# Two heads of a chunk in one step: the score and value products of three attentions in a two-block transformer kernel

## The chip, the cores and the metric

The kernel runs on one core of one Trainium2 chip. The metric is device microseconds of one execution of the whole program, as the median of three runs. A core has engines that run side by side, each with its own queue: TensorE (PE in the profile; its weight loads are PEld), VectorE (DVE), ScalarE (ACT), GpSimd (POOL) and SyncE (SP), whose queue mostly issues transfers. Products are written to PSUM, which has banks of 128 partitions x 512 float32; the kernel uses eight of them, two under each of the names `mm`, `s`, `t` and `o`.

## The reference, cut to what matters

Two transformer blocks on one sequence of T = 512 tokens of width 1024, all in float32. The change touches three attentions, all with heads of 64. Block 1 has a neighbourhood attention (8 heads on an 8 x 64 grid of tokens) and a dilated one (4 heads for each of 3 groups, whose results are mixed by their log-sum). Each of the two layers of block 2 has a sliding-window attention with sinks (8 query heads, 2 key heads), between two other attentions. For the sliding window:

```python
s = einsum('bnqgrd,bnkgd->bngrqk', qb, kb) * dh ** -0.5        # scores, 128 queries x 256 keys
s = where(mask, s, NEG_INF)
p = softmax(concatenate([s, sink], -1), -1)[..., :-1]
o = einsum('bngrqk,bnkgd->bnqgrd', p, vb)                      # values
```

The other two have the same form with other masks, and with a bias added to the scores. Everything else (projections, gates, feed-forward parts, two more attentions in each layer) consists of dense products and is not changed.

## The kernel before, in words

Tensors stand with features on partitions. A "chunk" is 128 features, hence two heads of 64: head 0 on partitions 0 to 63, head 1 on partitions 64 to 127. Dense products (`gemm`, L143 to L145; `vals`, L535 to L537) split each float32 operand in two float32r parts and add three products of 128 x 128 weights with up to 512 columns. Their weights arrive by transfers in SP's queue and are split by ACT (L88) and DVE (L89).

An attention step for 128 queries of one head goes: score product into a bank `s`; maximum (DVE, with the bias added), exponential and row sum (ACT); the reciprocal; `halves` (L98 ACT, L99 DVE), which scales the probabilities and writes them as two float16 parts; `turn` (L105), which transposes each 128 x 128 block by a product with the identity into a bank `t`; `copy` (L820 on ACT and L822 on DVE, in turn) to a tile `pts`; and the value product into a bank `o`. Score and value operands of the two attentions of block 1, and the value operands of the sliding window, are plain float32: the trace shows two PE instructions for each such product. The score products of block 1 contract over the 64 partitions of one head (`hs`), so they use 64 rows of the array. The value products write the 64 partitions of one head in `po`, so they use 64 of its columns. The sliding window's score products contract over 128 partitions (two parts of a key stacked) and use the whole array.

- Neighbourhood (`mix1`, loop over `c` in 4 chunks, `hp` in 2 heads, `cb` in 4 blocks of queries): one score product (L593) of 256 columns into its own bank, then softmax, two blocks turned, a 256-column copy, two value products (L609). The bias comes by one transfer for each head (L587) into a tile `bias` of which there are two. `vb` has six tiles, which hold the dilated attention's bias (L619) and values (L627 to L635).
- Dilated, `dil_scores(jp)` for two chunks: for each group `g` the heads one after the other; group 0 has 256 keys for each block of queries (L694, L698, L699; two blocks fill a bank), groups 1 and 2 have 128 (L692, four blocks to a bank). `dil_values(jp)`: head by head, 512 columns of turned blocks to a bank, one copy, four value products (L764).
- Sliding window (`swa`, called in both layers): head by head; scores of four blocks of queries (L1314 to L1319), softmax, then two banks of turned blocks (three and four blocks), two copies, and the value products (L1353). After each head a generator step lets one chunk of a dense product (`gates`) in.

The program is written as a sequence. A scheduler orders each engine's instructions ahead of time by a simulated timeline: those earlier in the program first, and later ones where an earlier one has to wait for its data or for a free tile. So dense products that come later in the text fill PE between the steps of an attention. On the chip the order of each engine is fixed. The change and the prediction speak of L593, L609, L692 to L699, L764, L1353, L98, L99, L105, L587, L619 and L635.

Of the kernel before, what the change touches and what calls it, by code (L numbers as in the profile page):

```python
# [17 lines left out]
T = 512  # L18
# [3 lines left out]
UP = 2.0 ** 15  # probabilities go through the turn times UP, values are divided by it  # L22
# [4 lines left out]
class Core:  # L27
# [13 lines left out]
    @contextmanager  # L41
    def phase(self, name, **tags):
        """a pool within the pools that are open: tag -> (bufs, floats to a partition)"""
        outer = self.tags
        with self.tc.tile_pool(name=name, bufs=1) as p:
            self.tags = {**outer, **{k: (p, *v) for k, v in tags.items()}}
            yield
        self.tags = outer

    def t(self, tag, dt=F32, n=None):  # L50
        """a tile of an open phase"""
        p, bufs, size = self.tags[tag]
        x = p.tile([128, size], dt, name=tag, tag=tag, bufs=bufs)
        return x if n is None else x[:, :n]
# [29 lines left out]
    # ---- exact split of float32 into two float32r parts  # L84
# [9 lines left out]
    def halves(self, P, scale, w=T):  # L94
        """P * scale as a sum of two float16 tiles"""
# [6 lines left out]
    def turn(self, out, hl, cols):  # L102
        """out = (h + l)[:, cols] transposed"""
# [3 lines left out]
    # ---- weights: DRAM -> SBUF -> (hi, lo)  # L107
# [4 lines left out]
    def pieces(self, raw, kc, n, where=None):  # L112
        """([hi], [lo]) of each row block; `where`: pairs of tags instead of the usual tiles"""
# [13 lines left out]
    def wcols(self, w, c0, n, k0=0, kc=8, where=None):  # L127
        """columns [c0, c0+n) of w rows [k0*128, (k0+kc)*128): list of pieces, 128 columns each"""
# [8 lines left out]
    def gemm(self, ps, w, xh, xl, cols=ALL):  # L137
        """ps[m, t] = sum_k w[k, m] x[k, t] for the tokens of cols; w = pieces, xh, xl lists of [128, T]"""
# [8 lines left out]
    # ---- rms statistics of feature-major chunks  # L147
# [26 lines left out]
        # first guess by halving the exponent, then Newton's steps  # L174
# [92 lines left out]
# ---------------------------------------------------------------- shape-only constants  # L267
# [50 lines left out]
class Block1(Core):  # L318
# [14 lines left out]
    def load_gains(self, a, names, eng):  # L333
        """one row per 128 features, turned to columns"""
# [23 lines left out]
    def load_x(self, x, gname):  # L358
        """chunks of x, features on partitions, and the norm that follows"""
# [101 lines left out]
    def gates(self, w, uh, ul, R, n, name):  # L461
        """tanh(gate / 2) of n feature chunks, to DRAM; sigmoid(z) = (1 + tanh(z / 2)) / 2; yields after each chunk"""
# [12 lines left out]
    def branch(self, gd, w, O, hl, merged, mtag="x"):  # L475
        """merged += (1 + tanh(gate / 2)) * (o @ w); yields after each chunk"""
# [30 lines left out]
    def mix1(self, X, U, a):  # L507
# [9 lines left out]
        def vals_w(c0, where=(None, None)):  # L517
            """weights of the values of 256 columns"""
# [5 lines left out]
        def vals(sets, dst, ms=range(4), held=None):  # L524
            """tokens on partitions, to dst [512, 256 a set] in DRAM"""
# [22 lines left out]
        # ---- A: neighbourhood  # L548
# [31 lines left out]
        self.narrow()  # L580
        for c in range(4):
            po = self.bank("o")
            for hp in range(2):
                h = 2 * c + hp
                hs = slice(hp * 64, hp * 64 + 64)
                bias = self.t("bias")
                nc.sync.dma_start(bias, self.na_bias.rearrange("r c h v k -> (r c) h (v k)")[:, h])  # L587
                bias = bias.rearrange("p (v k) -> p v k", v=3)
                k3 = K[c][hs].rearrange("p (r c) -> p r c", c=64)
                for cb in range(4):  # L590
                    st = self.small(tag="sa")
# [3 lines left out]
                    s = self.t("p")  # L595
                    nc.vector.tensor_tensor_reduce(s[:, 0:256], ps[:, 0:256], bias[:, BVAR[cb]], 1.0, -3e38,
                                                   OP.add, OP.max, st[:, 0:1])
                    p = self.expo(s[:, 256:512], s[:, 0:256], st)
                    nc.vector.reciprocal(st[:, 3:4], st[:, 2:3])
                    nc.vector.tensor_scalar(st[:, 3:4], st[:, 3:4], UP, None, op0=OP.mult)  # L600
                    hl = self.halves(p, st[:, 3:4], 256)
                    pt = self.bank("t")
                    for i in range(2):
                        blk = slice(i * 128, i * 128 + 128)
                        self.turn(pt[:, blk], hl, blk)
                    pts = self.t("pts")
                    self.copy(pts[:, 0:256], pt[:, 0:256])
                    for i in range(2):
                        nc.tensor.matmul(po[hs, cb * 128:(cb + 1) * 128], V[cb][:, i, h * 64:(h + 1) * 64],  # L609
                                         pts[:, i * 128:(i + 1) * 128], start=i == 0, stop=i == 1)  # L610
# [4 lines left out]
        # ---- B: dilated mixture  # L615
# [22 lines left out]
        def perm(ap, g):  # L638
            """natural token order seen in the order of group g"""
# [9 lines left out]
        def lviews(L, g, x):  # L649
            """[(partitions, DRAM view [p, 4, x])] of the token axis of L in the order of group g"""  # L650
# [7 lines left out]
        def dil_scores(jp):  # L658
# [14 lines left out]
            for g in range(3):  # L673
                both = None
                for hp in range(2):
                    hs = slice(hp * 64, hp * 64 + 64)
                    j = 2 * jp + hp
                    q, k = QB[g][hs], KB[g][hs]
                    kw = 256 if g == 0 else 128
                    if g == 0:  # L680
                        pt = self.t("vw")
                    else:
                        both = self.t("vw") if hp == 0 else both
                        pt = both[:, hp * 512:hp * 512 + 512]
                    P[g, hp] = pt = pt.rearrange("p (t k) -> p t k", t=4)
                    for t0 in range(0, 4, 512 // kw):
                        ps = self.bank("s").rearrange("p (t k) -> p t k", k=kw)
                        for ti in range(512 // kw):
                            t = t0 + ti
                            qt = q[:, t * 128:(t + 1) * 128]  # L690
                            if g:
                                nc.tensor.matmul(ps[:, ti], qt, k[:, t * 128:(t + 1) * 128], start=True, stop=True)  # L692
                            elif t in (1, 2):
                                nc.tensor.matmul(ps[:, ti], qt, k[:, 128 * t - 64:128 * t + 192], start=True, stop=True)  # L694
                            else:
                                e = k.rearrange("p (b t) -> p b t", t=64)[:, 0:8:7, :]
                                m = k[:, 64:192] if t == 0 else k[:, 320:448]
                                nc.tensor.matmul(ps[:, ti, 0:128], qt, e if t == 0 else m, start=True, stop=True)  # L698
                                nc.tensor.matmul(ps[:, ti, 128:256], qt, m if t == 0 else e, start=True, stop=True)  # L699
                        for ti in range(512 // kw):  # L700
# [5 lines left out]
                            else:  # L706
# [3 lines left out]
                                                           mx[:, g, t, hp:hp + 1])  # L710
                    nc.vector.tensor_scalar(neg[:, g, :, hp], mx[:, g, :, hp], -1.0, None, op0=OP.mult)
# [32 lines left out]
        def dil_values(jp, P, coef):  # L744
            for g in range(3):
                po = self.bank("o")
                nk = 2 if g == 0 else 1
                for hp in range(2):
                    hs = slice(hp * 64, hp * 64 + 64)
                    j = 2 * jp + hp  # L750
# [830 lines left out]
```

## Time and profile before

| | us |
|---|---|
| median of three runs (lowest, highest) | 3314.46 (3313.63, 3319.1) |
| span of the profiled execution | 3312.9 |
| PE busy in it | 3235.0 (98%) |
| DVE busy | 1913.5 (58%) |
| ACT busy | 1479.6 (45%) |
| mean granted clock of TensorE | 0.988 |
| neighbourhood attention | about 470 to 572 |
| dilated attention | about 588 to 746 |
| sliding windows of the two layers | about 1568 to 1656 and 2586 to 2676 |

The profile is of one execution. Its page gives each engine's busy time. The view by stretch gives the same for parts of the span, the view by line groups instructions of one line and shape, the view of waits tells which instruction of an engine waited for which other one, and the chain of waits follows the end of the program back in time. Along PE the chain gives one piece for each run of instructions of one line: when the piece began and how long it lasted until the next piece. A matmul's end in the trace is modelled, so a busy PE is not yet a PE at its peak, and the length of a chain piece says more than a matmul's own duration.

### The profile page before, as it was taken

The numbers are of one execution on the slowest core, as the hardware profiler recorded it, in microseconds if no ns is written. First come the engines' busy times: TensorE is split into PE (matmuls) and PEld (weight loads), VectorE is DVE, ScalarE is ACT, GpSimd is POOL, SyncE is SP. The second block draws the span as 40 slices with busy tenths as digits, with TensorE's granted clock in tenths as the row PEclk, the third lists the DMA queues.
The fourth block names the chain that finished last, engine by engine and source line by source line (L and its number), as shares of the span: only waits on it lengthen the run. The fifth ranks groups of instructions, "written<-read, shape, count | busy, mean of one in ns | idle before, by whom it ended". The sixth has DMA issues, their size and how long they took to land.

```text
span 3312.9 us, 45062 instructions
## 1 busy us (share of the span) xinstructions
PE 3235.0 (98%) x16815; PEld 2654.6 (80%) x16815; DVE 1913.5 (58%) x3749; ACT 1479.6 (45%) x2933; POOL 356.8 (11%) x562
## 2 busy tenths in 40 slices
PE   8999999999899998999999999999999999999998
PEld 7888887778888887788777888888778778788887
DVE  5344655545644457777676544356677667544355
ACT  4322344543432334677665422234577667322233
POOL 3100321101570011000003000000000002100001
PEclk9999999999999998999999999999899999999999
DMA  4432253235233324332355332324433345423222
GB/s 136 138 98 92 86 177 98 83 101 188 83 106 98 99 81 139 83 115 94 106 168 189 108 101 90 102 86 135 110 90 107 105 142 185 144 94 97 95 90 70
DMA packets 373930, 373.41 MB, mean 113 GB/s; under 512 B 48640, under 2 KB 326016, under 8 KB 373712
## 3 DMA queue, kind: packets, MB, share of 16 engines
q1 hardware_dynamic: 366864, 358.48, 35.1%
q0 software_dynamic: 6640, 12.01, 1.3%
q8 instruction: 132, 2.16, 0.3%
q14 instruction: 86, 0.70, 0.1%
q10 hardware_dynamic: 208, 0.05, 0.0%
HBM read 320.16 MB, written 44.91 MB: 110 GB/s over the span
## 4 chain that ended last, share of the span: by engine, by line
PE 90%; DVE 4%; DMA 3%; ACT 1%; issue 1%; SPq 0%; POOL 0%; DVEq 0%; ACTq 0%; POOLq 0%
PE ps_mm L143 13%; PE ps_mm L144 13%; PE ps_mm L145 13%; PE ps_t L143 6%; PE ps_t L145 6%; PE ps_t L144 6%; PE ps_s L145 6%; PE ps_s L143 6%; PE ps_s L144 6%; PE ps_s L956 2%; PE ps_t L982 2%; PE ps_t L105 1%; PE ps_o L989 1%; PE ps_o L990 1%; PE ps_o L1353 1%
## 5 line engine op out<-in xcount | busy, mean ns | idle before, releaser
L88 ACT ACTIVATE whi<-wraw 128x1024 fp32r<-128x1024 f32 (+3 forms) x518 | 503.8, 977 | 1157.1 <-PE ps_mm L144 352.1
L89 DVE TENSOR_TENSOR wlo<-wraw,whi 128x1024 fp32r<-128x1024 f32 (+3 forms) x518 | 595.6, 1152 | 173.7 <-ACT whi L88 168.2
L143 PE MATMUL ps_mm<-uh,whi 128*128 128x512 f32 (+1 forms) x1616 | 636.7, 394 | 3.6 <-DVE ft L1028 1.9
L145 PE MATMUL ps_mm<-uh,wlo 128*128 128x512 f32 (+1 forms) x1616 | 631.5, 391 | 0.0
L144 PE MATMUL ps_mm<-ul,whi 128*128 128x512 f32 (+1 forms) x1488 | 582.6, 392 | 3.1 <-DVE ul L92 3.1
L143 PEld LDWEIGHTS ps_mm<-uh,whi 128*128 128x128 f32 x1616 | 305.3, 189 | 61.3 <-DVE ft L1028 2.8
L145 PEld LDWEIGHTS ps_mm<-uh,wlo 128*128 128x128 f32 x1616 | 304.6, 189 | 56.3 <-issue 0.2
L144 PEld LDWEIGHTS ps_mm<-ul,whi 128*128 128x128 f32 x1488 | 281.1, 189 | 55.2 <-DVE ul L92 3.8
L143 PE MATMUL ps_t<-uh,whi 128*128 128x512 f32 (+1 forms) x632 | 243.7, 386 | 0.0
L145 PE MATMUL ps_t<-uh,wlo 128*128 128x512 f32 (+1 forms) x632 | 242.8, 384 | 0.0
L144 PE MATMUL ps_t<-ul,whi 128*128 128x512 f32 (+1 forms) x632 | 242.7, 384 | 0.0
L144 PE MATMUL ps_s<-ul,whi 128*128 128x512 f32 (+1 forms) x544 | 208.7, 384 | 0.0
L145 PE MATMUL ps_s<-uh,wlo 128*128 128x512 f32 (+1 forms) x544 | 208.6, 383 | 0.0
L143 PE MATMUL ps_s<-uh,whi 128*128 128x512 f32 (+1 forms) x544 | 208.4, 383 | 0.0
L99 DVE SCALAR_TENSOR_TENSOR ph<-p,sa,ph 128x128 f16<-128x128 f32 (+2 forms) x224 | 124.4, 561 | 28.9 <-ACT ph L98 26.6
L143 PEld LDWEIGHTS ps_t<-uh,whi 128*128 128x128 f32 x632 | 120.5, 191 | 22.7 <-DVE ul L92 0.2
L145 PEld LDWEIGHTS ps_t<-uh,wlo 128*128 128x128 f32 x632 | 120.4, 190 | 22.6
L144 PEld LDWEIGHTS ps_t<-ul,whi 128*128 128x128 f32 x632 | 120.4, 191 | 22.5
L98 ACT ACTIVATE ph<-p,sa 128x128 f16<-128x128 f32 (+2 forms) x224 | 121.9, 555 | 27.5 <-DVE sa L977 15.7
L956 PE MATMUL ps_s<-k,q 128*128 128x256 f32 (+1 forms) x448 | 131.0, 377 | 2.1 <-ACT p L961 1.7
L961 ACT ACTIVATE p<-ps_s,sa 128x128 f32<-128x128 f32 (+1 forms) x192 | 100.9, 529 | 50.0 <-DVE sa L960 34.8
L143 PEld LDWEIGHTS ps_s<-uh,whi 128*128 128x128 f32 x544 | 103.1, 190 | 19.5
(666 smaller groups left out, 6365.2 us busy)
## 6 DMA issues: line engine op xcount, KB each, us to landing
wraw<-w_in_in SPq DMA_DIRECT2D x28, 1024.0 KB, 5.4
wraw<-w_branch_gate_in SPq DMA_DIRECT2D x24, 1024.0 KB, 6.1
wraw<-ffn_w_gate_in SPq DMA_DIRECT2D x22, 1024.0 KB, 5.3
wraw<-ffn_w_up_in SPq DMA_DIRECT2D x22, 1024.0 KB, 5.3
wraw<-w_ffn_gate_in SPq DMA_DIRECT2D x22, 1024.0 KB, 6.1
wraw<-w_ffn_up_in SPq DMA_DIRECT2D x22, 1024.0 KB, 5.3
wraw<-ffn_w_down_in SPq DMA_DIRECT2D x24, 768.0 KB, 4.6
gates<-gt SPq DMA_DIRECT2D x64, 256.0 KB, 2.1
```

The source lines that it names most:

```text
L88: nc.scalar.activation(hi, src, AF.Copy)
L89: nc.vector.tensor_tensor(lo, src, hi.bitcast(F32), op=OP.subtract)
L98: self.nc.scalar.activation(h, P, AF.Copy, scale=scale)
L99: self.nc.vector.scalar_tensor_tensor(l, P, scale, h, op0=OP.mult, op1=OP.subtract)
L105: self.nc.tensor.matmul(out, hl[e][:, cols], self.ident16, start=e == 0, stop=e == 1)
L143: nc.tensor.matmul(o, w[0][k], xh[k][:, cols], start=k == 0, stop=False)
L144: nc.tensor.matmul(o, w[0][k], xl[k][:, cols], start=False, stop=False)
L145: nc.tensor.matmul(o, w[1][k], xh[k][:, cols], start=False, stop=k == kc - 1)
L956: nc.tensor.matmul(ps[:, 0:n], l, r, start=i == 0, stop=i == len(mms) - 1)
L961: nc.scalar.activation(P[:, 0:w], ps[:, 0:w], AF.Exp, bias=st[:, 0:1], accum_out=st[:, 1:2])
L982: nc.tensor.transpose(pt[:, e, k], hl[e][:, k * 128:k * 128 + 128], self.ident16)
L989: nc.tensor.matmul(o, v, PH[:, k], start=first and k == 0, stop=False)
```

## The change

Both heads of a chunk go through one step. In the neighbourhood attention a step takes two blocks of queries and both heads: two banks `s`, one for each head, four score products that alternate between the heads; then for each block of queries the softmax of both heads, four turned blocks in one full bank `t`, one copy of 512 columns, and four value products that alternate between the heads. `dil_scores` fills two banks `s` for the two heads of a group with alternating products, and then works through their softmax; `dil_values` turns the blocks of both heads into one bank and alternates their value products. `swa` takes the heads in pairs: scores and softmax of one, a generator step, scores and softmax of the other, then for each of the four blocks of queries the turns of both heads in one bank, one copy and the alternating value products.

Tiles: the neighbourhood's bias goes to `vb` and the tag `bias` is gone; `p` has four tiles instead of two, `ph` four instead of three; the norm at the end of `mix1` takes its two scratch tiles from `p`. The rest of the diff removes docstrings and comments.

```diff
 # mix1, neighbourhood
+        pair = tuple(slice(64 * e, 64 * e + 64) for e in range(2))
         for c in range(4):
             po = self.bank("o")
-            for hp in range(2):
-                bias = self.t("bias")
...
-                for cb in range(4):
-                    ps = self.bank("s")
-                    nc.tensor.matmul(ps[:, 0:256], Q[c][hs, cb * 128:(cb + 1) * 128],
-                                     k3[:, :, WSTART[cb]:WSTART[cb] + 32], start=True, stop=True)
...
+                b = self.t("vb", n=768)
...
+            for cb0 in range(0, 4, 2):
+                ps = [self.bank("s") for _ in pair]
+                for cb in (cb0, cb0 + 1):
+                    for hp, hs in enumerate(pair):
+                        nc.tensor.matmul(ps[hp][:, cb % 2 * 256:cb % 2 * 256 + 256], Q[c][hs, cb * 128:(cb + 1) * 128],
+                                         k3[hp][:, :, WSTART[cb]:WSTART[cb] + 32], start=True, stop=True)
+                for cb in (cb0, cb0 + 1):
                     pt = self.bank("t")
+                    for hp in range(2):
...
+                        hl = self.halves(p, st[:, 3:4], 256)
+                        for i in range(2):
+                            self.turn(pt[:, hp * 256 + i * 128:hp * 256 + i * 128 + 128], hl, slice(i * 128, i * 128 + 128))
+                    pts = self.t("pts")
+                    self.copy(pts, pt)
                     for i in range(2):
+                        for hp, hs in enumerate(pair):
+                            nc.tensor.matmul(po[hs, cb * 128:(cb + 1) * 128], V[cb][:, i, h * 64:(h + 1) * 64],
+                                             pts[:, hp * 256 + i * 128:hp * 256 + i * 128 + 128], start=i == 0, stop=i == 1)
 # dil_scores
+                for t0 in range(0, 4, 512 // kw):
+                    banks = [self.bank("s").rearrange("p (t k) -> p t k", k=kw) for _ in pair]
+                    def heads(ti, lo, w, t, keys):
+                        for ps, hs in zip(banks, pair):
+                            nc.tensor.matmul(ps[:, ti, lo:lo + w], QB[g][hs, t * 128:(t + 1) * 128], keys(KB[g][hs]),
+                                             start=True, stop=True)
...
 # dil_values
+                nt = 2 // nk
+                for t0 in range(0, 4, nt):
+                    pt = self.bank("t").rearrange("p (t h n q) -> p t h n q", t=nt, h=2, q=128)
...
+                    for ti in range(nt):
+                        for i in range(nk):
+                            for hp, hs in enumerate(pair):
                                 nc.tensor.matmul(po[hs, t * 128:(t + 1) * 128], VB[g][:, m, j * 64:(j + 1) * 64],
+                                                 pts[:, ti, hp, i], start=i == 0, stop=i == nk - 1)
 # swa
+        for h0 in range(0, 8, 2):
+            for h in (h0, h0 + 1):
...
+                kept.append((P, st))
+                if h == h0:
+                    yield
+            po = self.bank("o")
+            for j in range(4):
+                nk = 2 if j else 1
+                pt = self.bank("t")[:, 0:256 * nk].rearrange("p (h n q) -> p h n q", h=2, q=128)
+                for e, (P, st) in enumerate(kept):
+                    hl = self.halves(P[:, j, 0:128 * nk], st[:, 4, j:j + 1], 128 * nk)
+                    for n in range(nk):
+                        self.turn(pt[:, e, n], hl, slice(n * 128, n * 128 + 128))
...
+                for n in range(nk):
+                    for e, r in enumerate(rows):
+                        nc.tensor.matmul(po[r, j * 128:(j + 1) * 128], v, pts[:, e, n], start=n == 0, stop=n == nk - 1)
 # tiles of mix1
-            with k.phase("mix1", q=(10, 512), vb=(6, 1024), bias=(2, 768), p=(2, 512), pts=(2, 512), gt=(2, 512),
-                         ob=(2, 512), r8=(1, 512), sc=(6, 32), stats=(2, 72), ph=(3, 512)):
+            with k.phase("mix1", q=(10, 512), vb=(6, 1024), p=(4, 512), pts=(2, 512), gt=(2, 512),
+                         ob=(2, 512), r8=(1, 512), sc=(6, 32), stats=(2, 72), ph=(4, 512)):
```

## Rows read from the trace of the kernel before

**Rows 1.** The page: busy time of each engine, share, instructions.

```profile
PE 3235.0 (98%) x16815; PEld 2654.6 (80%) x16815; DVE 1913.5 (58%) x3749; ACT 1479.6 (45%) x2933; POOL 356.8 (11%) x562
```

**Rows 2.** By stretch: length, busy PE, PEld, DVE, ACT, POOL, clock, DMA share, GB/s.

```profile
470.00:572.00 102.00, 102.00 (x681) 79.23 (x680) 58.19 (x222) 53.55 (x136) 11.17 (x20) 1.00 0.33 98
588.00:746.00 158.00, 156.96 (x858) 121.60 (x857) 82.88 (x259) 78.02 (x201) 14.40 (x24) 1.00 0.30 91
1568.00:1656.00 88.00, 86.75 (x566) 67.22 (x563) 56.08 (x134) 57.67 (x150) 0.95 (x5) 1.00 0.33 99
2586.00:2676.00 90.00, 88.99 (x577) 68.88 (x577) 60.26 (x142) 59.22 (x156) 1.16 (x6) 1.00 0.32 100
```

**Rows 3.** PE by line and shape, block 1's attentions: count, busy us, mean ns.

```profile
L593 PE MATMUL ps_s<-q 64*128 64x256 f32 x64 | 20.2, 416 | 0.0
L609 PE MATMUL ps_o<-pts,vw 128*64 128x128 f32 x128 | 18.7, 281 | 0.0
L764 PE MATMUL ps_o<-pts,vb 128*64 128x128 f32 x128 | 17.4, 279 | 0.0
```

**Rows 4.** By stretch, PE alone, writing the banks `s`: the dilated scores.

```profile
588.00:652.00 64.00, 16.62 (x112) 1.00 0.27 80
```

**Rows 5.** PE by line and shape, both layers: the sliding windows' value products.

```profile
L1353 PE MATMUL ps_o<-p,v 128*64 128x128 f32 x224 | 30.1, 280 | 0.7 <-ACT p L820 0.7
```

**Rows 6.** The chain, pieces by start, length, what: neighbourhood scores, dense beside them.

```profile
474.39 0.12 PE ps_mm L535
474.50 0.63 PE ps_s L593 x2
475.13 0.31 PE ps_mm L536
...
485.15 1.06 PE ps_s L593 x4
```

**Rows 7.** The chain: neighbourhood values of one head, and the dense product behind.

```profile
519.99 0.58 PE ps_o L609 x4
520.57 0.31 PE ps_mm L537
```

**Rows 8.** The chain: dilated scores of two heads, of one head; two value instructions.

```profile
602.14 1.64 PE ps_s L692 x16
...
643.19 1.08 PE ps_s L692 x8
...
644.61 0.36 PE ps_o L764 x2
```

**Rows 9.** The chain: value products of the sliding window, runs of 6, 8, 14.

```profile
1587.14 0.80 PE ps_o L1353 x6
...
1593.86 1.02 PE ps_o L1353 x8
...
1605.69 1.29 PE ps_o L1353 x14
```

**Rows 10.** PE's waits in 470:746, 1568:1656, 2586:2676: for whom, us, times, longest.

```profile
PE ps_t L105 <- ACT ph L98: 0.8, 1, 0.8
PE ps_s L694 <- DVE stats L709: 0.3, 1, 0.3
...
PE ps_o L1353 <- ACT p L820: 0.7, 1, 0.7
...
PE ps_mm L143 <- DVE rt L1452: 1.0, 1, 1.0
```

**Rows 11.** ACT by line and shape, 470:572: exponential and scaling of one step.

```profile
L828 ACT ACTIVATE p<-p,sa 128x256 f32<-128x256 f32 x32 | 16.0, 500 | 6.8 <-DVE sa L827 6.6
L98 ACT ACTIVATE ph<-p,sa 128x256 f16<-128x256 f32 x32 | 15.8, 502 | 6.8 <-DVE sa L600 3.5 <-DVE sa L827 1.6 <-PE ps_t L105 1.4
```

**Rows 12.** Transfers into `vb` in 440:760: ns each, first and last start.

```profile
L635 POOL DMA_DIRECT2D vb<-dil_v x4: 553/558/576, 554.2 to 555.9; - x4
```

More of the change, by code (lines that the diff above doesn't have):

```diff
@@ L580, in mix1 @@
         self.narrow()
+        pair = tuple(slice(64 * e, 64 * e + 64) for e in range(2))
         for c in range(4):
             po = self.bank("o")
+            bias = []
             for hp in range(2):
[L584 to L589 removed]
@@ L673, in dil_scores @@
             for g in range(3):
-                both = None
-                for hp in range(2):
[L676 to L699, printed above, removed]
@@ new lines, in dil_scores, with ends, inner @@
+                kw = 256 if g == 0 else 128
+                if g == 0:
+                    pts = [self.t("vw") for _ in pair]
+                else:
+                    both = self.t("vw")
+                    pts = [both[:, hp * 512:hp * 512 + 512] for hp in range(2)]
+                pts = [x.rearrange("p (t k) -> p t k", t=4) for x in pts]
+                for t0 in range(0, 4, 512 // kw):
[4 more added lines that the diff above has]
+                                             start=True, stop=True)
+                    for ti in range(512 // kw):
+                        t = t0 + ti
+                        if g:
+                            heads(ti, 0, 128, t, lambda k: k[:, t * 128:(t + 1) * 128])
+                        elif t in (1, 2):
+                            heads(ti, 0, 256, t, lambda k: k[:, 128 * t - 64:128 * t + 192])
+                        else:
+                            def ends(k):
+                                return k.rearrange("p (b t) -> p b t", t=64)[:, 0:8:7, :]
+                            def inner(k):
+                                return k[:, 64:192] if t == 0 else k[:, 320:448]
+                            heads(ti, 0, 128, t, ends if t == 0 else inner)
+                            heads(ti, 128, 128, t, inner if t == 0 else ends)
+                    for hp in range(2):
+                        j = 2 * jp + hp
+                        pt, ps = pts[hp], banks[hp]
@@ L710, in dil_scores @@
                                                            mx[:, g, t, hp:hp + 1])
+                for hp in range(2):
+                    P[g, hp] = pt = pts[hp]
                     nc.vector.tensor_scalar(neg[:, g, :, hp], mx[:, g, :, hp], -1.0, None, op0=OP.mult)
@@ L803, in mix1 @@
         pw += self.wcols(a["w_out"][0], 768, 256, where=[[("p", "p"), ("ph", "ph")], [("rt", "rt"), ("rt", "pts")]])
-        step, U = self.post_norm(X, F, "mix_post_g", "ffn2_pre_g", "bias", "bias", "gt")
+        step, U = self.post_norm(X, F, "mix_post_g", "ffn2_pre_g", "p", "p", "gt")
         for cols in HALVES:
@@ new lines, in swa @@
+        rows = tuple(slice(64 * e, 64 * e + 64) for e in range(2))
+        for h0 in range(0, 8, 2):
+            g = h0 // 4
+            kept = []
+            for h in (h0, h0 + 1):
+                sc = 8 * i + h
+                st = self.small(20, "sa").rearrange("p (k j) -> p k j", k=5)
+                P = self.t("pp").rearrange("p (j k) -> p j k", j=4)
+                for pair in range(2):
+                    ps = self.bank("s").rearrange("p (j k) -> p j k", j=2)
+                    for jj in range(2):
+                        j = 2 * pair + jj
+                        q = Q[h][:, j * 128:(j + 1) * 128]
+                        k0 = 128 * max(j - 1, 0)
+                        nc.tensor.matmul(ps[:, jj], q, K[g][0][:, k0:k0 + 256], start=True, stop=False)
+                        if j:
+                            nc.tensor.matmul(ps[:, jj], self.identb, self.mask[:, 0:256], start=False, stop=False)
+                        else:
+                            nc.tensor.matmul(ps[:, jj, 0:128], self.identb, self.mask[:, 128:256], start=False, stop=False)
+                        nc.tensor.matmul(ps[:, jj], q, K[g][1][:, k0:k0 + 256], start=False, stop=True)
+                    if pair:
+                        nc.vector.tensor_reduce(st[:, 0, 2:4], ps, axis=AX.X, op=OP.max, negate=True)
+                    else:
+                        nc.vector.tensor_reduce(st[:, 0, 0:1], ps[:, 0, 0:128], axis=AX.X, op=OP.max, negate=True)
+                        nc.vector.tensor_reduce(st[:, 0, 1:2], ps[:, 1], axis=AX.X, op=OP.max, negate=True)
+                    s = slice(2 * pair, 2 * pair + 2)
+                    nc.vector.tensor_scalar(st[:, 1, s], st[:, 0, s], self.sink[:, 16 + sc:17 + sc], None, op0=OP.min)
+                    for jj in range(2):
+                        j = 2 * pair + jj
+                        n = 256 if j else 128
+                        nc.scalar.activation(P[:, j, 0:n], ps[:, jj, 0:n], AF.Exp, bias=st[:, 1, j:j + 1],
+                                             accum_out=st[:, 2, j:j + 1])
+                nc.scalar.activation(st[:, 3], st[:, 1], AF.Exp, bias=self.sink[:, sc:sc + 1])
+                nc.vector.tensor_tensor(st[:, 2], st[:, 2], st[:, 3], op=OP.add)
+                nc.vector.reciprocal(st[:, 4], st[:, 2])
+                nc.vector.tensor_scalar(st[:, 4], st[:, 4], UP, None, op0=OP.mult)
+                kept.append((P, st))
[9 more added lines that the diff above has]
+                        self.turn(pt[:, e, n], hl, slice(n * 128, n * 128 + 128))
+                pts = self.t("p")[:, 0:256 * nk].rearrange("p (h n q) -> p h n q", h=2, q=128)
+                self.copy(pts, pt)
+                for n in range(nk):
+                    kt = max(j - 1, 0) + n
+                    v = V[:, kt * 128 + 64 * g:kt * 128 + 64 * g + 64]
+                    for e, r in enumerate(rows):
+                        nc.tensor.matmul(po[r, j * 128:(j + 1) * 128], v, pts[:, e, n], start=n == 0, stop=n == nk - 1)
+            ot = self.t("oc", F32R), self.t("oc", F32R)
+            self.split(*ot, po)
+            self.store_o(ot, O[h0 // 2])
```

108 lines of the change are left out of this document (20 added, 88 removed).

## The prediction

> **What bounds the kernel now.** First the busy times of the page: PE is busy for 98% of the span, DVE for 58%, ACT for 45% [rows 1]. A busy PE need not be the bound, so next the stretches that hold the three attentions. There PE is busy for 102 of 102 us, 157.0 of 158, 86.8 of 88 and 89.0 of 90, at a granted clock of 1.00, with DVE at 52 to 67% and ACT at 49 to 66% [rows 2]. Then PE's waits in these stretches: 2.8 us in all [rows 10]. So PE never lacks work here, because dense products of later stages fill the time in which an attention computes its softmax. What the end depends on is how long PE takes for the sum of its instructions. Each us less in these stretches ends the program a us earlier, as long as DVE and ACT keep up.
>
> Next, what the narrow products cost. By line, the score products of the neighbourhood attention are 20.2 us of busy PE, its value products 18.7, the dilated ones 16.6 (scores) and 17.4 (values), the sliding window's value products 30.1 [rows 3 to 5]: 103.0 us. All of these use half of the array, as 64 rows or 64 columns.
>
> The chain then prices a run of them. Four value instructions of one head take 0.58 us [rows 7], six 0.80, eight 1.02 [rows 9]: 0.11 for each and some 0.14 to drain. And the dense product behind a run takes 0.31 where its neighbours take 0.12 [rows 6, 7]: going from half the array back to the whole one costs 0.19 more. I charge 0.15 for each run beside its chain piece, since many runs are followed by turns and not by a dense product; at 0.19 the sum below grows by 1.0 us.
>
> **Two heads do run beside each other, where they happen to meet.** In the sliding window there is a run of 14 instructions: the last eight of head 1 (columns 64 to 127) and the first six of head 2 (columns 0 to 63). By the price of one head it would take 1.02 + 6 x 0.11 = 1.68 us; it took 1.29 [rows 9]. In the dilated scores a run of 16, eight of each head (rows 0 to 63, then 64 to 127), should take 1.08 + 8 x 0.11 = 1.96 and took 1.64 [rows 8]. There are two of each, and both times the gain is some 3.5 instructions' worth, though the second head's come only at the end of the queue of the first. Where the heads alternate, I expect the overlap to be nearly whole: a run of two heads then takes as long as that of one.
>
> Here a rule of the Trainium skill speaks against half of this: "TensorE: Matmul & The Clock Gate", Part 3 (Packing small matmuls), lets a weight load overlap running products only where the row groups differ. Two value products share all rows and differ in columns alone, so by it they would gain nothing, which is rival B below. The run of 14 disagrees: it holds value products alone, with 14 weight loads, and is 0.39 us short of the serial price.
>
> What no row shows is two heads writing the same bank at once, since the heads in the run of 14 write two different `po`; in the changed kernel both write one `po`, each its own 64 partitions. From below this costs nothing (0.58 for a run of four and four), from above the serial 1.02; I take 0.58, because the partitions are apart and no row shows a bank holding a product up. The upper end is rival B.
>
> **The change part by part.** The count is of runs, each its chain piece + 0.15.
> - Neighbourhood scores. Before, 24 runs: 16 of two at 0.63 and 8 of four at 1.06 [rows 6], 18.6 + 3.6 = 22.2 us. After, 8 steps of four and four: 8 x (1.06 + 0.15) = 9.7. Saved 12.5.
> - Neighbourhood values. Before, 22 runs: 10 of eight at 1.02 and 12 of four at 0.58, 17.2 + 3.3 = 20.5. After, 16 runs of four and four at 0.73: 11.7. Saved 8.8.
> - Dilated scores. Before, twelve runs: two of 16 at 1.64, four of eight at 1.08 [rows 8], six of group 0 that come to 8.2 together; 15.8 + 1.8 = 17.6 (the 16.6 of [rows 4] is the same with modelled ends). After, 8 steps, each as long as one head's: 8 x (1.08 + 0.15) = 9.8. Saved 7.8.
> - Dilated values. Before, the worth of 16 runs of eight: 16 x 1.17 = 18.7. After, 16 runs of four and four: 11.7. Saved 7.0.
> - Sliding windows, both layers. Before, 30 runs (14 of six, 14 of eight, two of 14): 28.1 + 4.5 = 32.6. After, eight pairs of heads, each with three runs of four and four at 0.73 and one of two and two at 0.36 [rows 8] + 0.15: 8 x 2.70 = 21.6. Saved 11.0. Its score products use the whole array and stay as they are.
>
> Sum: 47.1 us.
>
> - Off the path: the 32 copies of 256 columns become 16 of 512; the counts of turns, halves and exponentials stay. ACT and DVE work beside PE here [rows 2], so I put this at nothing; were that cover gone, the copies would only be a gain.
> - Bias in `vb`. Eight bias loads, three table loads and three value loads now share six tiles, so tables and values of the dilated attention wait until earlier chunks' bias is read. They wait on SP's and POOL's queues, with weight loads queued behind them on SP and the value stores on POOL. The last one needs the fourth chunk to be done, near 570. In the kernel before, it is issued at 555.9 [rows 12], and the values are first used at 644.61 [rows 8]: some 70 us of room. The tables need the third chunk, near 546 (three quarters of 470 to 572), and are used from 588 on. Nothing, then; if the room were gone, it would be one transfer's time, a few us.
> - `p` and `ph` get more tiles, which can only remove waits: nothing.
>
> **What comes off the sum.** First, the banks. A step takes both banks `s`, so the next step's scores wait for both to be read. Head 0's bank comes free first, and a scheduler that sees one head ready may send it alone. In the dilated attention all of head 0 is read before head 1, so I give up the overlap in two or three of its eight steps (about 1 us each): 3 us. The Trainium skill points at the same place: "TensorEngine Tiling (Array Packing)", Restrictions and Gotchas, says that row tiling raises the pressure on PSUM and that different row tiles must not be in one bank at a time. Second, a joint step's value products need both heads' probabilities, and a faster PE meets ACT and DVE sooner: I double today's waits of 2.8 us [rows 10], 3 us more. So 47.1 - 6 = 41 us.
>
> The profiled span of 3312.9 us lies 1.6 under the median of 3314.46; the rest around it does not change. Forecast: 3314.5 - 41 = **3273.5 us**.
>
> **Rivals.**
> - A, the heads come apart in the scores: each head's products go when its own bank is free, with dense work between. Neighbourhood: 16 runs of four, 16 x 1.21 = 19.4, saved 2.8. Dilated: 16 runs at 1.23 = 19.7, lost 2.1. With the values' 26.8 and the 3 us of waits: 24.5 us, 3290. For it: two banks for two heads, and 16 of today's 24 runs are of one product. Against: the run of 16 went with both banks free [rows 8], and DVE, which reads them, is at 52 to 57% in these stretches [rows 2].
> - B, no overlap for value products (other columns, same rows, same bank): they run serially, 16 x 1.17 = 18.7 (saved 1.8), 18.7 (0), and 24 x 1.17 + 8 x 0.73 = 33.9 (lost 1.3). With the scores' 20.3 less 3, less 3 for waits: 14.8 us, 3300. Against: the run of 14.
> - C, the change doesn't do what it says: alternating products are kept apart by PE. Scores: 8 x (1.92 + 0.15) = 16.6 and 8 x 2.1 = 16.8, saved 6.4; values saved 0.5; less 3 for waits: 4 us, 3310.5. Against: both meeting runs.
> - D, slower: a joint step becomes a chain without cover. There are 64 value steps (16, 16 and 32). If at each of them PE had to sit through the second head's exponential and scaling on ACT, 0.50 + 0.50 us [rows 11], that is 64 us: 3273.5 + 64 = 3337.5. It decides against the change from 41 / 64 = 0.64 us a step on. For it: ACT is at 66% in the sliding windows already [rows 2], and a pair of heads is held back until both softmaxes are through. Against: PE waits 2.8 us in all today, as dense products stand ready in every stretch.
>
> **How the numbers follow.** Forecast 0.62; A 0.13; B 0.06; C 0.07; D 0.07; better than any loss allows, 0.05. The best case is half of the 103.0 us, 51.5, and a merged run or two: 3261. For 8 in 10 the range goes from there over the forecast, A and B, with a us for the charge at each end: 3261 to 3301. That leaves out C, D and the best case, 0.19. This kernel's measurement can tell some 0.2%, 6.6 us, from no change. Faster: forecast, A, B and the best case, 0.86; the same: C, 0.07; slower: D, 0.07.
>
> **What would show it.** In the chain, pieces of L609, L764 and L1353 x8 of some 0.6 us in place of 1.02, and score pieces x8 near 1.06 and x16 near 1.1; busy PE of these lines near 58 us (52.5 of pieces and 0.07 of modelled end for each of 80 runs) instead of 103. PE still busy for 97% or more of the four stretches, each shorter by what its lines lost. Rival A shows as score pieces of x4 and x8 with dense products between them; B as value pieces x8 of 1.02; C as the same in the scores; D as waits of L105, L609 or L1353 for ACT or DVE of some 0.6 us at each step. What would make the prediction wrong with all this in place: a schedule that shifts other stages, above all where PE already waits for transfers, or a stretch where dense products run out.

## The result, and the profile after

| | before | after |
|---|---|---|
| median, us (lowest to highest) | 3315.83 (3313.63 to 3319.1) | 3274.31 (3273.58 to 3275.7) |
| ratio, 95% interval | | 0.9873 (0.9862 to 0.9885) |
| span of the profiled execution | 3312.9 | 3273.9 |
| mean granted clock of TensorE | 0.988 | 0.984 |

The change takes 41.5 us off the median and 39.0 off the profiled span. The forecast was 3273.5. Timed once more beside the kernel before, the same kernel gave 3269.67 (ratio 0.9860, 0.9845 to 0.9875), so the size of the gain is known to some 5 us.

The page's busy times after, beside [rows 1]: PE has 36.2 us less of busy time and the same 16815 instructions.

```profile
PE 3198.8 (98%) x16815; PEld 2630.3 (80%) x16815; DVE 1909.7 (58%) x3741; ACT 1478.5 (45%) x2925; POOL 360.3 (11%) x562
```

The view by stretch (length, then busy PE, PEld, DVE, ACT, POOL, clock, DMA share, GB/s), cut to where the attentions now lie, beside [rows 2]: PE is still busy nearly throughout, with DVE at 59 to 79% and ACT at 57 to 76%.

```profile
471.00:530.00 59.00, 59.00 (x542) 49.60 (x540) 46.51 (x207) 44.67 (x120) 6.80 (x12) 1.00 0.32 99
571.00:702.00 131.00, 131.00 (x802) 100.78 (x801) 77.08 (x253) 74.65 (x197) 14.42 (x24) 1.00 0.35 100
1573.00:1630.00 57.00, 56.75 (x418) 42.48 (x417) 41.30 (x99) 38.07 (x101) 0.82 (x4) 1.00 0.37 107
2583.00:2637.00 54.00, 53.39 (x399) 39.97 (x397) 39.05 (x92) 35.56 (x96) 0.82 (x4) 1.00 0.33 106
```

PE by line and shape (count, busy us, mean ns), beside [rows 3 to 5]. L595 are the neighbourhood's scores, L615 its values, L692 the dilated scores, L777 the dilated values, L1367 the sliding windows' values. Together 63.7 us instead of 103.0.

```profile
L595 PE MATMUL ps_s<-q 64*128 64x256 f32 x64 | 13.6, 402 | 0.0
L777 PE MATMUL ps_o<-pts,vb 128*64 128x128 f32 x128 | 10.5, 284 | 0.0
L615 PE MATMUL ps_o<-pts,vw 128*64 128x128 f32 x128 | 9.0, 280 | 0.0
L692 PE MATMUL ps_s<-q 64*128 64x128 f32 x96 | 8.7, 287 | 0.0
L692 PE MATMUL ps_s<-q 64*128 64x256 f32 x16 | 3.3, 402 | 0.0
...
L1367 PE MATMUL ps_o<-p,v 128*64 128x128 f32 x224 | 18.6, 286 | 0.3 <-ACT p L833 0.3
```

The chain's pieces (start, us, what), beside [rows 6 to 9]:

```profile
476.57 1.07 PE ps_s L595 x8
...
482.25 1.06 PE ps_s L595 x4
483.62 1.06 PE ps_s L595 x4
485.70 1.02 PE ps_o L615 x16
...
523.25 0.59 PE ps_o L615 x8
...
591.20 1.10 PE ps_s L692 x16
...
621.65 1.64 PE ps_s L692 x16
...
634.82 0.59 PE ps_o L777 x8
```

Eight value instructions of two heads (x8; four products, since each is two instructions) take 0.59 us where eight of one head took 1.02 [rows 9], and sixteen take 1.02. Both heads write one bank here, so the point that no row of before showed is settled: it costs nothing. Eight score instructions of two heads take 1.07, as four of one did [rows 6]. But the pair at 482.25 and 483.62 is one step whose heads went apart, at 1.06 each. That happened in four of the neighbourhood's eight steps. In the dilated attention one step came apart, a second went in two runs, and in the run of 16 at 621.65 the second head's products all stand behind the first's, 1.64 instead of 1.10.

I sum, for each attention, its runs on PE from a run's start to the next instruction's, less what PE waits there, with the prediction's 0.15 for each run:

| us | before: runs, sum | forecast after | after: runs, sum | saved (forecast) |
|---|---|---|---|---|
| neighbourhood scores | 24, 22.1 | 9.7 | 12, 14.5 | 7.5 (12.5) |
| neighbourhood values | 22, 20.5 | 11.7 | 9, 9.7 | 10.8 (8.8) |
| dilated scores | 12, 17.6 | 9.8 | 10, 12.0 | 5.6 (7.8) |
| dilated values | 16, 18.7 | 11.7 | 15, 11.7 | 7.0 (7.0) |
| sliding windows' values | 30, 32.6 | 21.6 | 29, 21.1 | 11.4 (11.0) |
| sum | 104, 111.4 | 64.5 | 75, 69.1 | 42.3 (47.1) |

PE's idle time (span less its busy time) went from 77.9 to 75.1 us. TensorE's clock has two levels, 1.2 and 2.4 GHz. The clock rows of the trace put 67 us of busy PE at the lower one before and 85 us after. At half speed, half of that is lost: 33.6 and 42.5 us. So 42.3 of narrow products, plus 2.8 of idle time, less 8.9 of clock, is 36.2 of the 39.0 us. The rest lies in PE's other work. Without waits and as at the full clock, the dense products and the turns take 7.1 us less than before, where 0.15 for each of 29 runs less makes 4.4. PE comes to a dense product from a narrow run or from a turn 164 times before and 123 times after. A dense product of 512 columns takes 0.34 us from its start to the next one's behind a narrow run, 0.32 behind a turn, and 0.23 among its like (means after).

### The profile page after: what moved, and what is told of

Same layout as the page of the kernel before. It is cut to its first block, busy times and chain, and to the rows that moved or that the text cites. A ratio compares the mean times of both kernels' runs of the same rounds, so it can differ in the third digit from the quotient of the medians.

```text
span 3273.9 us, 45033 instructions
## 1 busy us (share of the span) xinstructions
PE 3198.8 (98%) x16815; PEld 2630.3 (80%) x16815; DVE 1909.7 (58%) x3741; ACT 1478.5 (45%) x2925; POOL 360.3 (11%) x562
## 4 chain that ended last, share of the span: by engine, by line
PE 90%; DVE 4%; DMA 3%; ACT 1%; issue 1%; SPq 0%; POOL 0%; DVEq 0%; ACTq 0%; POOLq 0%
PE ps_mm L143 13%; PE ps_mm L144 13%; PE ps_mm L145 13%; PE ps_t L143 6%; PE ps_t L145 6%; PE ps_t L144 6%; PE ps_s L143 6%; PE ps_s L145 6%; PE ps_s L144 6%; PE ps_s L969 2%; PE ps_t L995 2%; PE ps_o L1002 1%; PE ps_o L1003 1%; PE ps_t L105 1%; DVE x L407 1%
## 5 line engine op out<-in xcount | busy, mean ns | idle before, releaser
L144 PEld LDWEIGHTS ps_s<-ul,whi 128*128 128x128 f32 x544 | 102.6, 189 | 19.5
```

What stands on the lines that cost most here:

```text
L144: nc.tensor.matmul(o, w[0][k], xl[k][:, cols], start=False, stop=False)
```

## The experiments

e1 to e4 were timed side by side with the kernel before on one chip, u1 to u3 on a second, and e5 with e6 on a third. For each I give the median, the ratio with its interval, and a ledger of the profiled execution against that of the changed kernel: narrow runs (without the charge of 0.15), all other PE instructions (dense products and turns), both without waits and as at the full clock, then idle PE and what busy PE lost at half clock. The four make up the span. The last column counts how often PE comes to a dense product from a narrow run or a turn.

| us against the changed kernel | narrow | other PE | idle | clock | span | times (123 in the changed kernel) |
|---|---|---|---|---|---|---|
| e1 same rows | +9.0 | -1.8 | -3.0 | +1.8 | +6.0 | 123 |
| e2 head after head | +2.1 | +2.8 | +1.7 | -1.3 | +5.2 | 142 |
| e3 both banks | -5.7 | -1.7 | +1.7 | +3.5 | -2.1 | 119 |
| e4 long runs | -9.6 | -3.2 | +6.8 | +10.4 | +4.5 | 118 |
| u1 neighbourhood undone | +15.3 | +4.9 | +5.1 | +3.5 | +28.9 | 146 |
| u2 dilated undone | +11.6 | -1.9 | +1.1 | +0.3 | +11.1 | 115 |
| u3 windows undone | +12.3 | +3.4 | +1.8 | -2.3 | +15.1 | 141 |
| e5 changed again | 0.0 | 0.0 | -2.7 | -2.5 | -5.1 | 123 |
| e6 hold neighbourhood | -3.2 | +1.0 | +1.2 | -5.5 | -6.6 | 133 |

A profile is one execution of several. That of e4 is the longest of its four (3280.14 us; the others 3270.48 to 3276.45), that of u1 the second longest of six.

**Do the scores gain by the rows being different?** e1 gives both heads of block 1 the same 64 rows, in the same order of instructions (the second head's own scores are left out):

```diff
-  nc.tensor.matmul(ps[hp][...], Q[c][hs, cb * 128:(cb + 1) * 128], k3[hp][:, :, WSTART[cb]:WSTART[cb] + 32], ...)
+  nc.tensor.matmul(ps[hp][...], Q[c][0:64, cb * 128:(cb + 1) * 128], k3[0][:, :, WSTART[cb]:WSTART[cb] + 32], ...)
...
-  nc.tensor.matmul(ps[:, ti, lo:lo + w], QB[g][hs, t * 128:(t + 1) * 128], keys(KB[g][hs]), ...)
+  nc.tensor.matmul(ps[:, ti, lo:lo + w], QB[g][0:64, t * 128:(t + 1) * 128], keys(KB[g][0:64]), ...)
```

> The changed kernel, but the score products of both heads of block 1 read head 0's 64 partitions, so the second head's scores are head 0's again. Steps, banks, copies and the order on PE are those of the changed kernel; only the place in the array differs. Theory (the gain of the scores is that two heads run side by side on the two halves of the array's rows): the second head's products queue up behind the first's. The four joined runs of L595 go from 1.07 to 1.92 us, the joined runs of L692 from 1.08 and 1.10 to 1.95 and 1.96, two short ones lose 0.6 together: 8.4 us, 3282.7. Rival (the gain is that there are fewer and longer runs, and the place in the array does not matter): 3274.3.

Measured: 3280.82 us, ratio 0.9897 (0.9879 to 0.9915). The chain of e1, neighbourhood and dilated scores:

```profile
475.24 1.92 PE ps_s L595 x8
481.75 1.06 PE ps_s L595 x4
...
587.57 1.98 PE ps_s L692 x16
```

The joint runs go from 1.07 to 1.92 and from 1.10 to 1.98, and the runs of one head stay at 1.06. So the gain in the scores is the overlap of two halves of the rows, and it is 9.0 us here. The chain shows this; the time alone, though near the theory, does not, since e2 came to the same time with its scores unchanged.

**Must the value products alternate?** e2 puts the second head's behind the first's, inside each step; the neighbourhood's part of it is shown, the two others are alike:

```diff
-  for i in range(2):
-      for hp, hs in enumerate(pair):
+  for hp, hs in enumerate(pair):
+      for i in range(2):
```

> The changed kernel, but inside each step the value products of head 0 all come first, then those of head 1 (four and four instructions). Theory (PE starts a product for the free columns while up to three or so of the other head wait ahead of it, as in the runs of 14 and 16 of the kernel before): it is enough that the heads are neighbours in the queue; a run of four and four stays near 0.6 us, the whole near 3275. Rival (alternation is what brings the overlap): a run of four and four takes the serial 1.02 or close to it, 25.8 us more in 64 steps, 3300.

Measured: 3280.55 us, ratio 0.9895 (0.9876 to 0.9914). Its chain, neighbourhood values:

```profile
485.18 1.07 PE ps_o L615 x16
...
523.34 0.59 PE ps_o L615 x8
```

Four and four take 0.59 (0.594 on the mean against 0.590), sixteen 1.07 against 1.02. So for runs this short it is enough that both heads are in one run, and the rival's price of 1.02 did not come. The median is some 5 us above the theory, and so is the span: 2.1 us in the runs, and 2.8 in the other work, with 142 ways from a narrow run or turn to a dense product instead of 123. The order of the heads thus changed the schedule around the runs too.

**What does each attention give?** Three kernels put one attention's loops back to those of before, the rest left as changed (the neighbourhood's bias stays in `vb`). For u1:

```diff
-            for cb0 in range(0, 4, 2):
-                ps = [self.bank("s") for _ in pair]
...
+            for hp in range(2):
+                bias = self.t("vb", n=768)
...
+                for cb in range(4):
+                    ps = self.bank("s")
```

u2 does it with `dil_scores` and `dil_values`, u3 with `swa`.

> The changed kernel with the neighbourhood attention's loop head by head again (its bias still in the tag vb, four tiles p). In PE's order its scores are in 29 runs and its values in 28, more than in the kernel before. Theory (each run at its chain price and 0.15): 46.1 us against 24.3 now, 21.9 more, 3296. Rival (much of the gain comes from elsewhere, such as tiles or the schedule of other stages): under 8 us more.

> The changed kernel with the dilated attention's scores and values head by head again. Theory: 12 and 13 runs of 35.4 us against 23.8 now, 11.7 more, 3286. Rival (gain from elsewhere): under 4 us more.

> The changed kernel with the sliding window head by head again. Theory: 31 runs of 33.2 us against 21.0 now, 12.2 more, 3286.5. Rival (the pairing of heads has a price of its own, longer chains, that eats into its gain): under 4 us more.

Measured: 3300.99 (ratio 0.9947, 0.9932 to 0.9962), 3289.69 (0.9913, 0.9899 to 0.9926) and 3290.68 (0.9912, 0.9898 to 0.9926). As ratios against 0.9873 that is 24.5, 13.3 and 12.9 us lost, each uncertain by some 5 us. All three theories hold: each attention carries its share. The sum of 50.7 is more than the 41.5 of the whole. In u1, part of the excess is its schedule, in which the neighbourhood's products stand in 57 runs, against 46 before.

**Why did the heads come apart in the scores?** In e3, the first score product of a step waits for the last reading of both banks of the step before:

```diff
-                        nc.tensor.matmul(ps[hp][...], ..., start=True, stop=True)
+                        self.hold(nc.tensor.matmul(ps[hp][...], ..., start=True, stop=True), ...)
...
+                        if hp and cb % 2:
+                            self.held = read.ins
...
+    def hold(self, made, kind):
+        if self.held is not None:
+            self.tc.add_manual_dep(made.ins, self.held.name, ...)
+            self.held = None
```

> The changed kernel, with the first score product of a step made to wait until the last bank of the step before is read, so that no head goes alone. In the order of PE the neighbourhood's scores are then in 9 runs in place of 12, the dilated ones in 8 in place of 10, all runs together 69 in place of 75. Theory (steps whose heads came apart are where the scores' gain was lost): by the chain's prices 57.8 us of narrow runs become 52.1, and 6 runs less at 0.15: 6.6 us less, 3267.7. Rival (the wait for the second bank only moves the loss into PE's waits, or dense products fill less well): 3274 or more.

Measured: 3273.03 us, ratio 0.9869 (0.9851 to 0.9886). The neighbourhood's scores now stand in 9 runs instead of 12, 9.1 us of pieces instead of 12.7, and the dilated ones in 8 instead of 10. Seven of the neighbourhood's eight steps now go as one run, so what had parted them was that one bank came free before the other, as rival A has it. All narrow runs together take 52.2 us without waits (expected 52.1). The time did not follow: 1.7 us went into waits and 3.5 into the clock. The stretch of the dilated attention shows the waits:

```profile
571.00:702.00 131.00, 127.03 (x785) 99.03 (x784) 75.12 (x245) 74.07 (x197) 14.46 (x24) 0.99 0.32 99
```

PE is 4.0 us idle there where it had no idle time after the change alone. PE's waits of e3 in 560:720 (for whom, us, times, longest) name it:

```profile
PE ps_t L105 <- ACT ph L98: 2.8, 2, 2.1
PE ps_t L105 <- DVE ph L99: 0.9, 2, 0.5
PE ps_o L783 <- DVE pts L850: 0.2, 1, 0.2
```

The turns wait for the scaling on ACT and DVE: the mechanism of rival D, in a few places and brought on by the hold.

e4 adds to it that the values of two blocks of queries go in one run, behind the later copy, in all three attentions:

```diff
-                    self.copy(pts, pt)
-                    for i in range(2):
+                    copied = self.copy(pts, pt)
+                    turned.append(pts)
+                todo = []
+                for cb, pts in zip((cb0, cb0 + 1), turned):
...
+                self.run(copied, todo)
```

> As the run with both banks, and the value products of two blocks of queries are held until both blocks are copied and go as one run (eight and eight instructions, or six and six in the sliding window's first). 48 runs in place of 75. Theory (a run has a fixed price of some 0.15 beside its drain, whatever is in it): narrow runs 48.4 us in place of 57.8, and 27 runs less at 0.15: 13.4 us less, 3261. Rival (holding values back until the second copy leaves PE waiting or keeps tiles busy): no better than the run with both banks, 3268 or more.

Measured: 3275.43 us, ratio 0.9879 (0.9860 to 0.9897). PE's work did what was meant: 48 runs instead of 75, 9.6 us less in them and 3.2 in the other products. None of it arrives in the profiled execution. 6.8 us went into waits of PE (again 4 us in the dilated attention, in the sliding windows some 3), and 10.4 into the clock.

**Is the clock's part the order's doing?** Between 1200 and 1560 us (the end of the feed-forward part and the start of layer 1, up to the first scores of the sliding window, work that none of the three changes) the changed kernel and e4 issue the same 1978 PE instructions in the same order (in e3 one of them comes one place earlier), and yet e4 takes 6.2 us longer for them. e5 is the changed kernel once more; e6 holds the banks in the neighbourhood alone:

> The changed kernel itself, a second profile of it. Between 1200 and 1560 us the changed kernel and the two with held banks issue the same 1978 PE instructions in the same order, and yet the one with long runs took 6.2 us longer for them; its rows at half clock there cost 6.0 us more of busy PE. Theory: at which level the clock stands in the layers' first 150 us differs from execution to execution of one order, within some us. Then this profile's stretches at half clock between 1280 and 1400 differ from the 27 us of the first profile (17.1 + 3.4 + 6.8) by 3 us or more, and the span moves with them, by half of it; median 3274 within 4 us (ratio 0.9873 within 0.0012). Rival: the order alone sets the clock; then the stretches between 1280 and 1400 are again 17.1, 3.4 and 6.8 us, each in its place to 1 us, and the span is 3273.9 within 1 us.

> The changed kernel, with the first score product of a step held until both banks of the step before are read, in the neighbourhood attention alone. With both attentions held, the neighbourhood scores gained 4.0 us, and 3.9 us of waits of PE came in the dilated attention between 560 and 720. Theory: these waits come from the hold in the dilated attention, whose steps have nothing else to run. Then here PE waits under 1 us between 560 and 720, the neighbourhood scores take 8.7 us in place of 12.7, and the time is 4 us under the changed kernel of the same call: 3270, ratio 0.9861. Rival: the dense products that stand beside the attentions are a fixed stock, and what the neighbourhood attention no longer needs of PE's time is missing at the end of the dilated one: the 4 us come back as waits of L105 between 560 and 720, and the time stays that of the changed kernel, 3274.

e5: 3269.67 us, ratio 0.9860 (0.9845 to 0.9875). By stretch, the same instructions (from the first compression product of layer 1 on) in the changed kernel, in e5 and in e4; the edge of e5's stretch takes in one instruction more:

```profile
1297.70:1515.00 217.30, 213.85 (x1246) 170.92 (x1245) 160.24 (x409) 154.38 (x365) 9.03 (x51) 0.96 0.32 96
```

```profile
1292.40:1512.60 220.20, 217.15 (x1247) 173.50 (x1246) 160.37 (x409) 154.56 (x366) 9.02 (x51) 0.94 0.31 95
```

```profile
1296.50:1519.00 222.50, 218.96 (x1246) 175.14 (x1245) 160.13 (x409) 153.66 (x365) 9.14 (x51) 0.93 0.31 93
```

Length 217.3, 220.2 and 222.5 us at clocks of 0.96, 0.94 and 0.93. PE's idle time is the same (3.0 to 3.5), and all that PE does more of is to stand at the lower level: 2.9 and 5.2 us longer, where the clock rows make 3.8 and 5.8 us more loss. In the whole execution, e5 issues all 16815 instructions in the changed kernel's order and is 5.1 us shorter: 2.7 us of idle time, and 2.4 of busy PE, for which the clock rows at half speed make 2.5. So the theory on the clock holds in its first part: one order, two executions, and stretches at half clock between 1280 and 1400 of 27.3 and 37.5 us. Which chip the first of the two ran on is not on record, but one chip is enough for such differences: beside e1 to e4, seven executions of the kernel before have spans from 3308.8 us at a mean clock of 0.988 to 3318.7 at 0.985. Its second part fails: the span does not move with these stretches, since elsewhere less was lost (in block 1, 3.3 us against 7.4). The Trainium skill, "TensorE: Matmul & The Clock Gate", Part 1, says of the products at a kernel's start, which run at the lower clock, that their number and their duration vary from run to run of one kernel; these rows show a like variation in mid-kernel. Why the clock was lower for longer in e4 stays open: its four executions have mean clocks of 0.981 to 0.984, those of e1 to e3 beside them 0.983 to 0.987, so chance alone is not shown to be enough.

e6: 3268.2 us (3267.68 to 3269.1), ratio 0.9855 (0.9838 to 0.9871). PE has no wait at all between 560 and 720 us, so e3's 4 us of waits came from the hold in the dilated attention, and not from dense products that had run out: the rival falls. Of the 4 us expected, 1.5 show against e5 in the same comparison (lowest of e5 3269.01), which is 0.05% and hardly told apart. The profiles show where the rest went: up to the first product of layer 1, PE's work as at the full clock is 4.2 us less than in e5, but 4.5 us more are lost at the lower clock (7.8 against 3.3). e6 has the lowest median of the study. Its neighbourhood scores go jointly, but for one step in two runs:

```profile
477.05 1.06 PE ps_s L595 x8
482.94 1.06 PE ps_s L595 x8
...
502.71 1.06 PE ps_s L595 x6
503.18 0.59 PE ps_o L619 x8
503.76 0.63 PE ps_s L595 x2
```

## Why the prediction was right, step by step

- **What bounds the kernel.** "Each us less in these stretches ends the program a us earlier" held for block 1: its narrow runs lost 30.9 us, and the first product of layer 1's own projections (L1086) starts 30.5 us earlier, at 1208.2 instead of 1238.7. In the layers it held less well: 11.4 us of runs, 8.5 of time, with 6.2 us more lost at the lower clock there.
- **Two heads overlap whole.** Forecast 0.58 for four and four, measured 0.59; 1.06 for the scores, measured 1.06 to 1.07; e1 shows what it is without (1.92). Rivals B and C are out. The rule of the Trainium skill, "TensorE: Matmul & The Clock Gate", Part 3, that was weighed against it does not hold for columns here: in the run of 0.59 us, value products of all rows and different columns overlap, and so do their eight weight loads. One reading behind this step was loose: the run of 16 of [rows 8] gained 0.32 us, three instructions' worth and not 3.5.
- **The scores, mis-sized.** The step "I give up the overlap in two or three of its eight steps (about 1 us each): 3 us" was too small and in the wrong place. The dilated scores lost 2.2 us of the forecast, as allowed, and the neighbourhood's 5.0, for which nothing was allowed: rival A came true there in half of the steps. The scores together saved 13.1 where 17.3 was left after the allowance.
- **The values, mis-sized the other way.** I counted one run for each step. The schedule put two steps' values in one run seven times in the neighbourhood (16 in 1.02 us, where two runs cost 1.46 with the charge): 2.0 us more than forecast. The sliding windows gave 0.4 more.
- **The charge, mis-sized.** "I charge 0.15 for each run" counts narrow runs alone. But dense products behind turns are slower too (0.32 us instead of 0.23), and PE comes to them from turns 96 times instead of 124. In all, PE's other work gave 7.1 us, 0.24 for each of the 29 runs less, which is 2.7 more than the charge.
- **The waits.** "I double today's waits of 2.8 us" did not come: in the four stretches above, which are narrower than those of [rows 10], PE waits 0.7 us in all (1.5 with those just beside them, in 1560:1640 and 2570:2645), against 2.8, and its idle time in the whole span fell by 2.8. Rival D is out for this kernel, and e3 shows that it is near: one more dependency in the dilated attention cost 4 us.
- **The clock.** It was no term of the sum: 8.9 us more lost than before. One profile of each kernel does not tell how much of this is the change's. Two executions of one order differ by 2.5 us, and the profile of before is one with little loss: its mean clock is 0.988, where 25 other executions of that kernel have 0.984 to 0.988.
- **Bias in `vb`, `p` and `ph`, the copies.** Put at nothing, and no wait of PE for any of them is in the four stretches.

So the mechanism of the forecast was right and most of its gain came from where it said, while the terms around it missed by -4.2 (scores), +2.0 and +0.4 (values), +2.7 (charge), +5.8 (waits and idle) and -8.9 (clock). These nearly cancel; the wait term had the wrong sign, and the clock was not foreseen. That the forecast came within 0.8 us of the median is therefore partly luck: the narrow products were to give 44.1 us after the allowance for the banks, and gave 42.3, and the second timing of the same kernel was 4.6 us lower.

## What to carry to other kernels

Small products that use half of the array are worth pairing by the other half, and a run of both costs what one costs: price them by run, as its chain piece plus what the way in and out costs, and merge runs where nothing has to wait for it. Count the ways back from turns as well. When a step takes two buffers that come free one after the other, look in the schedule whether it still goes as one step. And before a gain of a few us is believed or missed, compare two executions of one order: here they differ by as much.

## What the runs showed that I had not expected

- Alternation is not needed for the overlap in a short run: four and four, head after head, take 0.59 us. In longer ones it matters: score runs of 16 took 1.64 us with eight of one head before eight of the other, and 1.10 alternating.
- One kernel, the same order of all 16815 PE instructions, and spans of 3273.9 and 3268.8 us on two occasions, while the times of each occasion stayed inside 2.1 and 1.5 us.
- A stretch of 217 to 222 us in which PE works on the same instructions and is idle 3.0 to 3.5 us in each lost 8.3, 12.1 or 14.1 us at the lower clock by the clock rows.
